# Mean of the squares by a constant matrix, and a stacked low-rank gate, in a hybrid decoder layer

## The chip, the cores and the metric

The kernel runs on one core of a Trainium2 chip. The metric is the device time of one execution, in microseconds (us). Engines are named as in the profile: PE (TensorE's products) and PEld (its weight loads), DVE (VectorE), ACT (ScalarE), POOL (GpSimd), SP (SyncE, which issues nearly all DMAs).

## What is computed

One decoder layer on 256 tokens of 1024 channels, float32: a mixer (gated linear attention beside causal pooling), a layer norm, a mixture of 64 experts with a shared one, a second layer norm. The change touches two places of the attention branch:

```python
# the gate: a product of rank 16, then one up to 512 channels
log_decay = log_sigmoid(einsum('bsr,rk->bsk', g_lr, w_gate_up) + b_gate) / 16
...
# each head's output (256 channels) over the root of its mean square
def rms_norm(x, g):
    y = x * lax.rsqrt(jnp.square(x).mean(-1, keepdims=True) + RMS_EPS)
    return y * g
o = rms_norm(o, gla_norm_g).reshape(B, S, GLA_DV)
o = o * silu(r)
```

## The kernel before

**Stages.** The mixer comes first (to some 215 us of the span), then routing, then 32 steps of two experts each, whose weights stream in through rings of 1 MB buffers. All instructions are issued in the order in which the program writes them, engine by engine; no scheduler moves them.

**Projections.** The input weights come in 22 chunks of 256 columns (q, k, v, r, u, ga, gb; buffers `w_0` to `w_21`), each handled as halves. A half is first *split*: ACT writes a rounded copy `sh` (type float32r, L296), DVE the rest `sl` (L297). Then PE runs 24 products on it: L300 (`sh` with the rounded x), L301 (`sh` with x's rest), L302 (`sl` with the rounded x). The loop `run` issues the split of a half two places ahead of its products (`LOOK = 2`), and `between` behind each half's products issues one step of the background generators: `pool_steps` and the chain `gla_steps`, `out_steps`, `gate_steps`. So work of the attention and pooling branches stands in every engine's queue between the splits and products of the halves.

**The gate.** Behind chunk q0 comes the piece `g`: `split_to(wg, ...)` makes the rounded and the rest part of the rank-16 weights side by side (`wgs`, 32 columns), and `rank_mm` (L615) multiplies them with both parts of x: 16 float32r products into 32 rows of `pg` (L620, L621). ACT copies these to `glr` in float32. After the next half, `gla_steps` multiplies `wgu` (the up weights, loaded twice so that 32 rows add both parts) with `glr`: four products in plain float32 (L366), which the trace shows as 8 passes, into `plog`.

**The heads' norms.** `out_steps` (L488) has a step for each of the four heads: products `po` (L503, L504); then `square_sums` of the head before: two float32 products with the squares `sq` as weights and a column of ones, giving one number for each token, tokens on partitions (`psq`, L495); ACT squares (L508), POOL adds the two halves of the channels (L509), ACT writes the scaled output `oT` (L513). After the last head ACT takes the root of the 128x8 sums (L516) and DVE the reciprocal (L517). Since the outputs lie with channels on partitions, the roots are then spread over all partitions by products with the identity, four for two heads (`prs`, L535), and DVE multiplies `oT` by silu(r) (L527) and by `prs` (L528), which it reads from PSUM. `pool_steps` goes on beside this: DVE's `pl` (L557 to L559), one product `pm` (L553), DVE's `mx`.

**POOL at the start.** Its queue holds a cast of the identity, a cast `trib` of constants that a DMA brings (L280), memsets of `A0`, `A1` (L345, L346) and, from `gla_steps`, of `B` (L373).

Of the kernel before, what the change touches and what calls it, by code (L numbers as in the profile page):

```python
# [5 lines left out]
FT = mybir.dt.float32  # L6
FR = mybir.dt.float32r
BF = mybir.dt.bfloat16
I32 = mybir.dt.int32
AF = mybir.ActivationFunctionType  # L10
# [3 lines left out]
T, D = 256, 1024  # L14
H, DK, DV = 4, 128, 256
# [95 lines left out]
def body(ctx, tc, A, out, dbg=lambda *a: None, stop=None):  # L111
    nc = tc.nc
    ctx.enter_context(tc.manual_schedule())
    PE, V, S, G = nc.tensor, nc.vector, nc.scalar, nc.gpsimd
# [94 lines left out]
    ident = cst[:, C_ID:C_ID + 128]  # L209
# [24 lines left out]
    right = tc.alloc_tile_pool(name="right", bufs=1, side="right")  # L234
    gla = tc.alloc_tile_pool(name="gla", bufs=1)
    onesb = right.tile([128, 128], BF, name="onesb")
    cst1 = right.tile([128, C_COLS - C_KEPT], FT, name="cst1")

    def cst_of(c, n):
# [4 lines left out]

    x = ring1.tile([128, 2048], FT, name="x", tag="w1", bufs=NR1).rearrange("p (t d) -> p t d", t=2)
    wg = gla.tile([128, 8, 16], FT, name="wg")
    wgu = gla.tile([32, 512], FT, name="wgu")
    wgrp = right.tile([128, 4, 128], FT, name="wgrp")
    nc.scalar.dma_start(ident, A["cst"][:, C_ID:C_ID + 128])
    halves = [slice(0, 512), slice(512, 1024)]  # L250
# [5 lines left out]
    ring.midway = lambda: load_x(1)  # L256
    ring.issue(ring1, "w1", NR1)
    nc.sync.dma_start(wg, w_in[:, 3072:3088].rearrange("(k p) c -> p k c", p=128))
    for n in range(2):
        nc.sync.dma_start(wgu[16 * n:16 * n + 16], A["w_gate_up"][0])  # L260
    nc.sync.dma_start(bgate, A["b_gate"][0].rearrange("(h p) -> p h", p=128))
    ring.issue(ring1, "w1", NR1)
    nc.sync.dma_start(cst1, A["cst"][:, C_KEPT:])
# [11 lines left out]
    V.memset(eps_rms, RMS_EPS)  # L275
    V.memset(eps_ln, LN_EPS)
    V.memset(onesb, 1.0)
    V.memset(ones1, 1.0)
    G.tensor_copy(identb, ident)
    G.tensor_copy(trib, cst_of(C_TRI, 128))  # L280
# [14 lines left out]
    def split_to(src, hi, lo, eng=V):  # L295
        S.activation(hi, src, AF.Copy)  # L296
        eng.tensor_sub(lo, src, hi.bitcast(FT))  # L297
# [39 lines left out]

    qT = gla.tile([128, H, T], FT, name="qT")
    kT = gla.tile([128, H, T], FT, name="kT")
    glr = gla.tile([32, T], FT, name="glr")  # L340
    wgs = gla.tile([128, 8, 2, 16], FR, name="wgs")
    v = right.tile([128, 2, D], FT, name="v")
    A0 = right.tile([128, H, 256], FT, name="A0")
    A1 = right.tile([128, H, 128], FT, name="A1")
# [12 lines left out]
    pools, L = {}, {}  # L357

    def gla_steps():
        yield  # L360
        xb = gla.tile([128, H, T], FT, name="E", bufs=2)
        for hp in range(2):
            p = bank("b", (2, T), "plog")
            for h2 in range(2):
                h = 2 * hp + h2
                PE.matmul(p[:, h2], wgu[:, 128 * h:128 * (h + 1)], glr, start=True, stop=True)  # L366
            for h2 in range(2):
                h = 2 * hp + h2
                V.tensor_scalar(xb[:, h], p[:, h2], bgate[:, h:h + 1], None, op0=OP.add)
# [116 lines left out]
        yield  # L486

    def out_steps():  # L488
        oTs = {}
        psq = bank("b", (2, H), "psq")  # L490
        rs = right.tile([128, 2, H], FT, name="rs")

        def square_sums(h):
            for t in range(2):
                PE.matmul(psq[:, t, h:h + 1], L["sq", h][:, 128 * t:128 * (t + 1)], one_c,  # L495
                          start=h == 0 and t == 0, stop=True, skip_group_check=True)

        yield ("v", 3)
        for h in range(H):
# [13 lines left out]
                S.activation(oT[:, c], p[:, c], AF.Copy, scale=gnorm[:, c:c + 1])  # L513
            yield
        square_sums(H - 1)
        S.activation(rs, psq, AF.Sqrt, bias=eps_rms, scale=1.0 / DV)  # L516
        V.reciprocal(rs, rs)  # L517
        yield ("r", 3)
        og, prs = {}, {}
        for i in range(H + 2):  # L520
            if i >= 2:
                hs = slice(2 * i - 4, 2 * i - 2)
                split_to(og[i - 2], L["ogh"][:, hs], L["ogl"][:, hs], eng=G)
            if 1 <= i <= H:
                h = i - 1
                og[h] = right.tile([128, 2, T], FT, name="og", tag="og", bufs=2)
                V.tensor_mul(og[h], oTs[h], rT[:, 2 * h:2 * h + 2])  # L527
                V.tensor_mul(og[h], og[h], prs[h // 2][:, h % 2, None, :].to_broadcast([128, 2, T]))  # L528
            if i < H:
                S.activation(rT[:, 2 * i:2 * i + 2], rT[:, 2 * i:2 * i + 2], AF.Silu)  # L530
                if i % 2 == 0:
                    prs[i // 2] = bank("b", (2, T), "prs")
                    for h2 in range(2):
                        for t in range(2):
                            PE.matmul(prs[i // 2][:, h2, 128 * t:128 * (t + 1)],  # L535
                                      rs[:, t, i + h2:i + h2 + 1].to_broadcast([128, 128]), ident,
                                      start=True, stop=True)
            yield

    def pool_steps():  # L540
# [74 lines left out]
    def rank_mm():  # L615
        pg = bank("b", (T,), "pg")

        for k in range(8):
            w = wgs[:, k].rearrange("p a r -> p (a r)")
            PE.matmul(pg[:32], w, xTh[:, k], start=k == 0, stop=False)  # L620
            PE.matmul(pg[:32], w, xTl[:, k], start=False, stop=k == 7)  # L621
        S.activation(glr, pg[:32], AF.Copy)

    pieces = []
    for name, c, _ in chunk_cols:
        st = {}
        parts = 4 if (name, c) == ("q", 0) else 2
        for part in range(parts):
            if len(pieces) == 1:
                pieces.append((("x", 0, True), lambda: None, lambda: x_part(1)))  # L630
            pieces.append(((name, c, part == parts - 1),) + proj_piece(name, c, part, parts, st))
        if (name, c) == ("q", 0):
            pieces.append((("g", 0, 1), lambda: split_to(wg, wgs[:, :, 0], wgs[:, :, 1]), rank_mm))

    def done(key):
        finished.add(key)
# [695 lines left out]
```

## Time and profile before

| | |
|---|---|
| time before, median of 3 runs | 690.85 us (690.08 to 690.96) |
| the profiled execution: its own time, its span | 691.21 us, 689.4 us |
| PE, PEld busy share of the span | 97%, 68% |
| DVE, ACT, POOL | 42%, 33%, 10% |
| mean DMA rate over the span | 351 GB/s |
| chain that ended last, by engine | PE 25%, DMA 13%, DVE 1% |

The profiled execution is one run under the hardware profiler; its span runs from the first to the last instruction, and its own time holds 1.8 us around that. The shares are means over stages that differ, so a stage is read from its own stretch. Matmul durations overlap (they are pipelined), so what a product costs is read from one start to the next.

### The profile page before, as it was taken

The numbers are of one execution on the slowest core, as the hardware profiler recorded it, in microseconds if no ns is written. First come the engines' busy times: TensorE is split into PE (matmuls) and PEld (weight loads), VectorE is DVE, ScalarE is ACT, GpSimd is POOL, SyncE is SP. The second block draws the span as 40 slices with busy tenths as digits, with TensorE's granted clock in tenths as the row PEclk, the third lists the DMA queues.
The fourth block names the chain that finished last, engine by engine and source line by source line (L and its number), as shares of the span: only waits on it lengthen the run. The fifth ranks groups of instructions, "written<-read, shape, count | busy, mean of one in ns | idle before, by whom it ended". The sixth has DMA issues, their size and how long they took to land. (4 is left out here: it accounts for less than half of the span.)

```text
span 689.4 us, 13660 instructions
## 1 busy us (share of the span) xinstructions
PE 668.5 (97%) x5940; PEld 471.8 (68%) x5940; DVE 287.8 (42%) x458; ACT 227.8 (33%) x348; POOL 66.8 (10%) x53
## 2 busy tenths in 40 slices
PE   8999999999999999999999999999999999798994
PEld 8999999999999756556546546556645655464531
DVE  3698845946676522123123123324431321231216
ACT  4654546674445213123123113311311321131222
POOL 1064404600002000000000002100000000100001
PEclk9999999999999999999999999999999999999997
DMA  9995533499677999999999999999999999999991
GB/s 283 308 349 163 180 123 124 142 385 420 249 265 299 348 421 381 422 420 419 418 419 421 420 419 419 411 420 421 418 420 422 418 421 417 421 419 417 408 328 64
DMA packets 66885, 242.02 MB, mean 351 GB/s; under 512 B 7012, under 2 KB 36452, under 8 KB 43016
## 3 DMA queue, kind: packets, MB, share of 16 engines
q1 hardware_dynamic: 66680, 241.07, 89.2%
q8 instruction: 47, 0.77, 0.5%
q10 hardware_dynamic: 144, 0.07, 0.1%
q14 instruction: 14, 0.11, 0.0%
HBM read 240.07 MB, written 1.05 MB: 350 GB/s over the span
## 5 line engine op out<-in xcount | busy, mean ns | idle before, releaser
L1033 PE MATMUL pgu<-w,xg 128*64 128x256 f32 x1840 | 222.4, 381 | 1.3 <-DMA w<-in_w_exp_gate 1.3
L1033 PEld LDWEIGHTS pgu<-w,xg 128*64 128x64 f32 x1840 | 138.7, 137 | 86.1 <-ACT Y L1063 11.7
L1058 PE MATMUL py<-w,ht 128*32 128x512 f32 (+1 forms) x912 | 120.2, 580 | 1.8 <-DMA w<-in_w_exp_down 1.4
L297 DVE TENSOR_TENSOR sl<-w,sh 128x1024 fp32r<-128x1024 f32 (+1 forms) x63 | 80.3, 1281 | 40.3 <-ACT sh L296 40.1
L1040 DVE TENSOR_TENSOR h<-sg,pgu 128x256 f32<-128x256 f32 x32 | 13.5, 422 | 191.3 <-ACT sg L1039 147.0
L1064 DVE SCALAR_TENSOR_TENSOR Y<-py,gsl,Y 128x512 fp32r<-128x512 f32 (+1 forms) x66 | 48.5, 735 | 102.1 <-ACT Y L1063 102.0
L1063 ACT ACTIVATE Y<-py,gsl 128x512 fp32r<-128x512 f32 (+1 forms) x66 | 44.5, 674 | 116.1 <-PE py L1058 116.1
L300 PE MATMUL proj<-xTh,sh 128*128 128x256 f32 x288 | 82.0, 285 | 0.3 <-ACT sh L296 0.3
L301 PE MATMUL proj<-xTl,sh 128*128 128x256 f32 x288 | 80.6, 280 | 0.0
L302 PE MATMUL proj<-xTh,sl 128*128 128x256 f32 x288 | 80.3, 279 | 0.2 <-DVE sl L297 0.2
L1039 ACT ACTIVATE sg<-pgu 128x256 f32<-128x256 f32 x32 | 12.3, 384 | 201.6 <-PE pgu L1033 201.6
L296 ACT ACTIVATE sh<-w 128x1024 fp32r<-128x1024 f32 (+1 forms) x63 | 64.2, 1027 | 32.8 <-PE proj L302 12.6
L1058 PEld LDWEIGHTS py<-w,ht 128*32 128x32 f32 x912 | 30.5, 109 | 55.0 <-issue 46.9
L300 PEld LDWEIGHTS proj<-xTh,sh 128*128 128x128 f32 x288 | 54.1, 188 | 1.1 <-ACT sh L296 0.5
L301 PEld LDWEIGHTS proj<-xTl,sh 128*128 128x128 f32 x288 | 54.1, 188 | 0.3 <-DVE xTl L297 0.2
L302 PEld LDWEIGHTS proj<-xTh,sl 128*128 128x128 f32 x288 | 54.0, 187 | 0.4 <-DVE sl L297 0.4
L1058 PE MATMUL py<-xTh,ht 128*32 128x512 f32 x80 | 36.3, 594 | 0.0
L1033 PE MATMUL pgu<-xTl,xg 128*64 128x256 f32 x128 | 29.2, 381 | 3.8 <-DMA xTl<-in_w_exp_up 3.8
L786 DVE TENSOR_SCALAR xg<-pgat,cols_sb 128x512 f32<-128x512 f32 x32 | 25.7, 809 | 13.9 <-PE pgat L914 11.4
L914 PE MATMUL pgat<-P,xl 128*128 128x256 f32 x128 | 30.6, 283 | 0.3 <-DVE xl L950 0.3
L788 ACT ACTIVATE xg<-pgat,cols_sb 128x512 f32<-128x512 f32 x32 | 24.7, 778 | 17.3 <-PE pgat L914 17.3
L914 PE MATMUL pgat<-P,xh 128*128 128x256 f32 x128 | 30.3, 283 | 0.0
(271 smaller groups left out, 950.7 us busy)
## 6 DMA issues: line engine op xcount, KB each, us to landing
w<-in_w_exp_gate SPq DMA_DIRECT2D x62, 1024.0 KB, 15.9
w<-in_w_exp_up SPq DMA_DIRECT2D x53, 1024.0 KB, 16.8
w<-in_w_exp_down SPq DMA_DIRECT2D x47, 1024.0 KB, 19.8
w<-in_w_in SPq DMA_DIRECT2D x21, 1024.0 KB, 7.0
xTl<-in_w_exp_up SPq DMA_DIRECT2D x7, 1024.0 KB, 15.6
w<-in_w_exp_down SPq DMA_DIRECT2D x12, 512.0 KB, 14.8
xTh<-in_w_exp_down SPq DMA_DIRECT2D x5, 1024.0 KB, 19.8
w<-in_w_gla_up SPq DMA_DIRECT2D x4, 1024.0 KB, 10.8
```

The lines of the kernel that those rows point to most:

```text
L296: S.activation(hi, src, AF.Copy)
L297: eng.tensor_sub(lo, src, hi.bitcast(FT))
L300: PE.matmul(o, ah, bh, start=start, stop=False, skip_group_check=shared_bank)
L301: PE.matmul(o, ah, bl, start=False, stop=False, skip_group_check=shared_bank)
L302: PE.matmul(o, al, bh, start=False, stop=stop, skip_group_check=shared_bank)
L786: V.tensor_scalar(dst, p, g1T[:, k:k + 1], b1T[:, k:k + 1], op0=OP.mult, op1=OP.add)
L788: S.activation(dst, p, AF.Identity, bias=b1T[:, k:k + 1], scale=g1T[:, k:k + 1])
L914: PE.matmul(p[k][:, t].rearrange("p e s -> p (e s)"), part[:, t, k], P8[o][:, t].rearrange("p e s -> p (e s)"), start=part is xh, stop=par ...
L1033: PE.matmul(p[64 * c:64 * c + 64, g], xg[:, k, e].rearrange("p t s -> p (t s)"), w[c][:, k], start=k == 0, stop=k == 7, tile_position=(0, ...
L1058: PE.matmul(p[32 * c:32 * c + 32], HT[2 * q + c // 2][:, j, c % 2, t], ring.get(li["down", 4 * q + c])[:, j, cs], start=j == 0, stop=j == ...
L1063: S.activation(hi, p, AF.Copy, scale=g)
L1064: V.scalar_tensor_tensor(lo, p, g, hi.bitcast(FT), op0=OP.mult, op1=OP.subtract)
```

## The change

The gate: the up weights are loaded six times by one DMA, into 96 rows. The first product's weights are written three times side by side (POOL copies them, in the new `split_rank`), so that it gives the low-rank rows three times, in 96 rows. Of these the first 64 are kept rounded (`glr`, now float32r) and the last 32 hold the rest; of the up weights rows 32 to 63 hold the rest and the others the rounded part (`wgr`). One float32r product over 96 rows then adds the three partial products.

The norms: a 128x128 matrix of 1/256 is the weight, and a head's squares move past it, so that the mean of each token arrives on all partitions at once. Two heads share a bank; after the second, ACT takes the root and DVE the reciprocal of 128x512, in place of rows of `A0` that are no longer needed, and DVE multiplies by them from there. The products that spread the roots are gone.

```diff
--- before.py
+++ after.py
@@ -234,6 +234,7 @@
     right = tc.alloc_tile_pool(name="right", bufs=1, side="right")
     gla = tc.alloc_tile_pool(name="gla", bufs=1)
     onesb = right.tile([128, 128], BF, name="onesb")
+    mean = right.tile([128, 128], FT, name="mean")
     cst1 = right.tile([128, C_COLS - C_KEPT], FT, name="cst1")
 
     def cst_of(c, n):
@@ -244,7 +245,8 @@
 
     x = ring1.tile([128, 2048], FT, name="x", tag="w1", bufs=NR1).rearrange("p (t d) -> p t d", t=2)
     wg = gla.tile([128, 8, 16], FT, name="wg")
-    wgu = gla.tile([32, 512], FT, name="wgu")
+    wgu = gla.tile([96, 512], FT, name="wgu")
+    wgr = gla.tile([96, 512], FR, name="wgr")
     wgrp = right.tile([128, 4, 128], FT, name="wgrp")
     nc.scalar.dma_start(ident, A["cst"][:, C_ID:C_ID + 128])
     halves = [slice(0, 512), slice(512, 1024)]
@@ -256,8 +258,8 @@
     ring.midway = lambda: load_x(1)
     ring.issue(ring1, "w1", NR1)
     nc.sync.dma_start(wg, w_in[:, 3072:3088].rearrange("(k p) c -> p k c", p=128))
-    for n in range(2):
-        nc.sync.dma_start(wgu[16 * n:16 * n + 16], A["w_gate_up"][0])
+    six = bass.AP(tensor=A["w_gate_up"].tensor, offset=A["w_gate_up"].offset, ap=[[0, 6], [512, 16], [1, 512]])
+    nc.sync.dma_start(wgu, six)
     nc.sync.dma_start(bgate, A["b_gate"][0].rearrange("(h p) -> p h", p=128))
     ring.issue(ring1, "w1", NR1)
     nc.sync.dma_start(cst1, A["cst"][:, C_KEPT:])
@@ -275,6 +277,7 @@
     V.memset(eps_rms, RMS_EPS)
     V.memset(eps_ln, LN_EPS)
     V.memset(onesb, 1.0)
+    V.memset(mean, 1.0 / DV)
     V.memset(ones1, 1.0)
     G.tensor_copy(identb, ident)
     G.tensor_copy(trib, cst_of(C_TRI, 128))
@@ -337,8 +340,8 @@
 
     qT = gla.tile([128, H, T], FT, name="qT")
     kT = gla.tile([128, H, T], FT, name="kT")
-    glr = gla.tile([32, T], FT, name="glr")
-    wgs = gla.tile([128, 8, 2, 16], FR, name="wgs")
+    glr = gla.tile([96, T], FR, name="glr")
+    wgs = gla.tile([128, 8, 3, 2, 16], FR, name="wgs")
     v = right.tile([128, 2, D], FT, name="v")
     A0 = right.tile([128, H, 256], FT, name="A0")
     A1 = right.tile([128, H, 128], FT, name="A1")
@@ -363,7 +366,7 @@
             p = bank("b", (2, T), "plog")
             for h2 in range(2):
                 h = 2 * hp + h2
-                PE.matmul(p[:, h2], wgu[:, 128 * h:128 * (h + 1)], glr, start=True, stop=True)
+                PE.matmul(p[:, h2], wgr[:, 128 * h:128 * (h + 1)], glr, start=True, stop=True)
             for h2 in range(2):
                 h = 2 * hp + h2
                 V.tensor_scalar(xb[:, h], p[:, h2], bgate[:, h:h + 1], None, op0=OP.add)
@@ -486,14 +489,18 @@
         yield
 
     def out_steps():
-        oTs = {}
-        psq = bank("b", (2, H), "psq")
-        rs = right.tile([128, 2, H], FT, name="rs")
+        oTs, psq, prs = {}, {}, {}
 
         def square_sums(h):
-            for t in range(2):
-                PE.matmul(psq[:, t, h:h + 1], L["sq", h][:, 128 * t:128 * (t + 1)], one_c,
-                          start=h == 0 and t == 0, stop=True, skip_group_check=True)
+
+            if h % 2 == 0:
+                psq[h // 2] = bank("b", (2, T), "psq")
+            PE.matmul(psq[h // 2][:, h % 2], mean, L["sq", h], start=True, stop=True)
+            if h % 2:
+
+                prs[h // 2] = rs = A0[:, h - 1:h + 1]
+                S.activation(rs, psq[h // 2], AF.Sqrt, bias=eps_rms)
+                V.reciprocal(rs, rs)
 
         yield ("v", 3)
         for h in range(H):
@@ -513,10 +520,8 @@
                 S.activation(oT[:, c], p[:, c], AF.Copy, scale=gnorm[:, c:c + 1])
             yield
         square_sums(H - 1)
-        S.activation(rs, psq, AF.Sqrt, bias=eps_rms, scale=1.0 / DV)
-        V.reciprocal(rs, rs)
         yield ("r", 3)
-        og, prs = {}, {}
+        og = {}
         for i in range(H + 2):
             if i >= 2:
                 hs = slice(2 * i - 4, 2 * i - 2)
@@ -528,13 +533,6 @@
                 V.tensor_mul(og[h], og[h], prs[h // 2][:, h % 2, None, :].to_broadcast([128, 2, T]))
             if i < H:
                 S.activation(rT[:, 2 * i:2 * i + 2], rT[:, 2 * i:2 * i + 2], AF.Silu)
-                if i % 2 == 0:
-                    prs[i // 2] = bank("b", (2, T), "prs")
-                    for h2 in range(2):
-                        for t in range(2):
-                            PE.matmul(prs[i // 2][:, h2, 128 * t:128 * (t + 1)],
-                                      rs[:, t, i + h2:i + h2 + 1].to_broadcast([128, 128]), ident,
-                                      start=True, stop=True)
             yield
 
     def pool_steps():
@@ -615,11 +613,19 @@
     def rank_mm():
         pg = bank("b", (T,), "pg")
 
+
         for k in range(8):
-            w = wgs[:, k].rearrange("p a r -> p (a r)")
-            PE.matmul(pg[:32], w, xTh[:, k], start=k == 0, stop=False)
-            PE.matmul(pg[:32], w, xTl[:, k], start=False, stop=k == 7)
-        S.activation(glr, pg[:32], AF.Copy)
+            w = wgs[:, k].rearrange("p n a r -> p (n a r)")
+            PE.matmul(pg[:96], w, xTh[:, k], start=k == 0, stop=False)
+            PE.matmul(pg[:96], w, xTl[:, k], start=False, stop=k == 7)
+        S.activation(glr, pg[:96], AF.Copy)
+        V.tensor_sub(glr[64:96], pg[64:96], glr[64:96].bitcast(FT))
+        S.activation(wgr, wgu, AF.Copy)
+        V.tensor_sub(wgr[32:64], wgu[32:64], wgr[32:64].bitcast(FT))
+
+    def split_rank():
+        split_to(wg, wgs[:, :, 0, 0], wgs[:, :, 0, 1])
+        G.tensor_copy(wgs[:, :, 1:3], wgs[:, :, 0:1].to_broadcast([128, 8, 2, 2, 16]))
 
     pieces = []
     for name, c, _ in chunk_cols:
@@ -630,7 +636,7 @@
                 pieces.append((("x", 0, True), lambda: None, lambda: x_part(1)))
             pieces.append(((name, c, part == parts - 1),) + proj_piece(name, c, part, parts, st))
         if (name, c) == ("q", 0):
-            pieces.append((("g", 0, 1), lambda: split_to(wg, wgs[:, :, 0], wgs[:, :, 1]), rank_mm))
+            pieces.append((("g", 0, 1), split_rank, rank_mm))
 
     def done(key):
         finished.add(key)
```

On POOL, at the start of the program: `trib` is the cast of constants, `A_210`/`A_211` are A0 and A1, `wgs` the first product's weights. Before:

```order
L279 CAST identb<-cst 128x128 [waits DMAHW0_49]
L280 CAST trib<-cst_97 128x128 [waits DMAHW4_49]
L345 MEMSET A_210 128x1024
L346 MEMSET A_211 128x512
L373 MEMSET B 128x1024
L458 ISA
```

and now:

```order
L282 CAST identb<-cst 128x128 [waits DMAHW0_49]
L283 CAST trib<-cst_98 128x128 [waits DMAHW3_49]
L348 MEMSET A_212 128x1024
L349 MEMSET A_213 128x512
L628 COPY wgs<-wgs 128x8x64 [waits DVE_49]
L376 MEMSET B 128x1024
```

A copy of 128x8x64 stands behind the two memsets, and the memset of `B` behind it; the first of the gate's products now waits for POOL where it waited for DVE.

On DVE, from the third head's step to the second step of the pool branch (`w_15`, `w_16` are the second and third ga chunk). Before:

```order
L297 TENSOR_TENSOR sl<-w_15_917,sh 128x1024 [waits DMAHW2_49,Activation_49]
L297 TENSOR_TENSOR sl<-w_15_917,sh 128x1024 [waits PE_49,Activation_49]
L557 SCALAR_TENSOR_TENSOR pl<-sw,uT 128x256 [waits Pool_49]
L558 TENSOR_TENSOR pl<-sw,cst_97 128x16 [waits DVE_49]
L559 TENSOR_TENSOR pl<-pl,uT 128x16 [waits DVE_49]
L517 RECIPROCAL rs<-rs 128x8 [waits Activation_49]
L297 TENSOR_TENSOR sl<-w_16_1021,sh 128x1024 [waits DMAHW3_49,PE_49,Activation_49]
L557 SCALAR_TENSOR_TENSOR pl<-sw,uT 128x256 [waits Pool_49]
L558 TENSOR_TENSOR pl<-sw,cst_97 128x16 [waits DVE_49]
L559 TENSOR_TENSOR pl<-pl,uT 128x16 [waits DVE_49]
L297 TENSOR_TENSOR sl<-w_16_1021,sh 128x1024 [waits PE_49,Activation_49]
```

and now:

```order
L503 RECIPROCAL A_212<-A_212 128x512 [waits Activation_49]
L300 TENSOR_TENSOR sl<-w_15_923,sh 128x1024 [waits DMAHW1_49,Activation_49]
L300 TENSOR_TENSOR sl<-w_15_923,sh 128x1024 [waits PE_49,Activation_49]
L555 SCALAR_TENSOR_TENSOR pl<-sw,uT 128x256 [waits Pool_49]
L556 TENSOR_TENSOR pl<-sw,cst_98 128x16 [waits DVE_49]
L557 TENSOR_TENSOR pl<-pl,uT 128x16 [waits DVE_49]
L503 RECIPROCAL A_212<-A_212 128x512 [waits Activation_49]
L300 TENSOR_TENSOR sl<-w_16_1027,sh 128x1024 [waits DMAHW2_49,PE_49,Activation_49]
L555 SCALAR_TENSOR_TENSOR pl<-sw,uT 128x256 [waits Pool_49]
L556 TENSOR_TENSOR pl<-sw,cst_98 128x16 [waits DVE_49]
L557 TENSOR_TENSOR pl<-pl,uT 128x16 [waits DVE_49]
L300 TENSOR_TENSOR sl<-w_16_1027,sh 128x1024 [waits PE_49,Activation_49]
```

A reciprocal of 128x512 stands before the first `sl` of `w_15`, and the one behind the first `pl` triple, ahead of `w_16`, grows from 128x8 to 128x512.

## Rows read from the trace of the kernel before

**Rows 1.** Busy time of the engines by stretch: us, PE, PEld, DVE, ACT, POOL, PEclk, DMA share, GB/s

```profile
112.00:140.00 28.00, 28.00 (x234) 27.79 (x234) 23.70 (x34) 19.69 (x29) 13.76 (x13) 1.00 0.46 156
180.00:215.00 35.00, 35.00 (x231) 32.04 (x230) 23.79 (x30) 15.23 (x23) 5.10 (x2) 1.00 0.62 215
240.00:600.00 360.00, 354.85 (x3018) 205.66 (x3014) 99.37 (x174) 80.33 (x138) 9.65 (x6) 1.00 1.01 418
```

**Rows 2.** Timeline of PE late in the experts: start us, us, engine, line, what [idle before]

```profile
656.97 0.43 PE L1033 MATMUL pgu<-xTl,xg 128*64 128x256 f32 x1 [1.20 <-DMA xTl<-in_w_exp_up]
```

**Rows 3.** Timeline of PE around the gate's two products

```profile
15.51 0.28 PE L620 MATMUL pg<-xTh,wgs 128*32 128x256 f32 x1
...
17.35 0.28 PE L300 MATMUL proj<-xTh,sh 128*128 128x256 f32 x1
...
19.95 0.28 PE L302 MATMUL proj<-xTh,sl 128*128 128x256 f32 x1
20.16 1.99 PE L366 MATMUL plog<-glr,wgu 32*128 32x256 f32 x8
...
22.30 0.28 PE L301 MATMUL proj<-xTl,sh 128*128 128x256 f32 x1
```

**Rows 4.** Timeline of POOL in the same stretch

```profile
14.57 0.29 POOL L280 CAST trib<-cst 128x128 bf16<-128x128 f32 x1 [10.56 <-DMA cst<-in_cst]
...
15.69 0.53 POOL L346 MEMSET A<- 128x512 f32 x1
16.16 0.96 POOL L373 MEMSET B<- 128x1024 f32 x1
```

**Rows 5.** POOL's largest plain copy, from the costliest groups: busy us, mean ns

```profile
L919 POOL CAST xh<-x 128x1024 fp32r<-128x1024 f32 x1 | 2.1, 2149 | 72.4 <-DVE x L779 72.4
```

**Rows 6.** Columns as in rows 1, the microsecond in which the constants land

```profile
14.00:15.00 1.00, 1.00 (x11) 1.00 (x10) 0.00 (x0) 0.95 (x1) 0.42 (x2) 1.00 1.10 347
```

**Rows 7.** Timeline of PE: square sums of one head, and one spreading of the roots

```profile
99.62 0.50 PE L495 MATMUL psq<-small,sq 128*128 128x1 f32 x4
99.99 0.36 PE L300 MATMUL proj<-xTh,sh 128*128 128x256 f32 x1
...
115.34 0.59 PE L553 MATMUL pm<-pl,wgrp 128*128 128x256 f32 x2
115.77 1.05 PE L535 MATMUL prs<-cst,rs 128*128 128x128 f32 x8
116.58 0.36 PE L300 MATMUL proj<-xTh,sh 128*128 128x256 f32 x1
```

**Rows 8.** Timeline of DVE from the last head to the second gb half

```profile
113.02 0.41 DVE L557 SCALAR_TENSOR_TENSOR pl<-sw,uT 128x256 f32<-128x256 f32 x1
...
113.67 0.18 DVE L559 TENSOR_TENSOR pl<-pl,uT 128x16 f32<-128x16 f32 x1
...
115.42 1.23 DVE L297 TENSOR_TENSOR sl<-w,sh 128x1024 fp32r<-128x1024 f32 x1 [0.74 <-ACT sh L296]
...
118.32 1.23 DVE L297 TENSOR_TENSOR sl<-w,sh 128x1024 fp32r<-128x1024 f32 x1 [0.91 <-ACT sh L296]
...
133.42 1.61 DVE L297 TENSOR_TENSOR sl<-w,sh 128x1024 fp32r<-128x1024 f32 x1
```

**Rows 9.** Timeline of PE: first product that uses that last sl

```profile
136.05 0.28 PE L302 MATMUL proj<-xTh,sl 128*128 128x256 f32 x1
```

**Rows 10.** Reciprocals of eight elements and of one: duration ns min/median/max, first and last start us

```profile
L517 DVE RECIPROCAL rs<-rs x1: 203/203/203, 114.5 to 114.5; 128x8 f32<-128x8 f32 x1
L778 DVE RECIPROCAL mv<-mv x2: 164/164/165, 208.0 to 215.1; 128x1 f32<-128x1 f32 x2
L1261 DVE RECIPROCAL mv<-mv x2: 151/158/164, 679.1 to 682.2; 128x1 f32<-128x1 f32 x2
```

**Rows 11.** The two multiplications of a head's og, columns as in rows 10

```profile
L527 DVE TENSOR_TENSOR og<-oT,rT x4: 684/758/1107, 120.6 to 131.9; 128x512 f32<-128x512 f32 x4
L528 DVE TENSOR_TENSOR og<-og,prs x4: 686/687/689, 121.4 to 132.8; 128x512 f32<-128x512 f32 x4
```

## The prediction

> **What bounds the kernel now.** I read the stretches first, then the chain that ended last, then the timelines of the places the change touches. In the stretches [rows 1] PE is busy 28.00 of 28 us between 112 and 140, and 35.00 of 35 between 180 and 215, while the DMA engines are at 0.46 and 0.62 of their time. From 240 to 600 the DMA share is 1.01. So the mixer is bound by PE, and the experts by the weight stream, which PE meets again at the end: at 656.97 it has stood 1.20 us for a transfer [rows 2]. The stream starts late because its buffers come free as PE gets on, so each microsecond that PE gains or loses in the mixer should move the whole end by as much. The change is priced in PE's time before 215 us, and another engine's work counts only where PE waits for it. DVE is the one to watch: busy 23.70 of 28 us where the heads' roots are used [rows 1].
>
> **The second product of the gate.** Before, it is 8 float32 passes. From the last projection product ahead of it (19.95) to the second one behind it (22.30) PE needs 2.35 us [rows 3]. After, it is four products of 128x256 in one pass each. The first product of the gate is in that form and takes 1.84 us for 16, from 15.51 to 17.35, so 0.115 each [rows 3]. With the two projection products that stand in the 2.35 us, six of them take 0.69. The saving is 2.35 - 0.69 = **1.66 us**. The first product keeps its 16 instructions and 256 columns; it writes 96 rows instead of 32. The projection piece behind it writes 128 rows and starts its 24 products between 17.35 and 19.95, 2.60/23 = 0.113 each [rows 3], so I cost the added rows at nothing.
>
> **The copies of its weights.** They are made on POOL, behind two memsets and a cast of constants that waits for a load. The constants land at 14.57, and POOL is free only at 16.16, when it begins the memset of B [rows 4]; the new copy takes that place. PE wants the weights at 15.51 [rows 3], so it must wait. Two terms stand on bounds. The copy is 128x512. A memset of that shape takes 0.53 [rows 4]; the only copy to the product's type, of twice the length, takes 2.15, half of which is 1.08 [rows 5]. I take 0.8, the middle. The gate's up weights are loaded six times in one DMA instead of twice in two, 128 KB more, ahead of the constants in a queue whose engines are already full (share 1.10, 347 GB/s [rows 6]): 0.38 us later, or nothing if the one DMA issue saved lets the queue start as much earlier. I take 0.38. Then PE starts at 16.16 + 0.38 + 0.8 = 17.34, a wait of **1.83 us**, between 1.18 and 2.11. If POOL were free, the wait would vanish.
>
> The new ACT and DVE steps (the copy of the low-rank rows in 96 rows, the rounded weights, two subtractions) lie between the two products, where PE works on a projection piece from 17.35 to 20.16, 2.8 us [rows 3]. Three of them in series at the 0.69 of a 128x512 multiplication [rows 11] are 2.1 us: covered, with 0.7 to spare; without cover they would cost what exceeds 2.8. The memset of the mean matrix stands before the warm-up products, which only fill time before x lands: nothing, and at worst 0.53 [rows 4].
>
> **The mean and the roots.** A head's sums take PE 0.37 us before (99.62 to 99.99 [rows 7]). After, they are one float32 product of 128x256, two passes; such a pair takes 0.43 (115.34 to 115.77 [rows 7]). Four heads: 4 x 0.06 = **+0.24 us**. Spreading the roots, 0.81 us (115.77 to 116.58 [rows 7]), is removed; it occurs twice: **-1.62 us**. So PE wins 1.38 us here if nobody makes it wait. The ACT roots grow from 128x8 to two of 128x512, and the order has as many table loads as before; ACT is busy 19.69 of 28 us [rows 1], so I cost them at nothing.
>
> DVE pays. Its reciprocals grow from 8 elements to 512, twice. The row of 8 took 203 ns, those of one element 164 and at best 151 [rows 10]. The slope is 39/7 = 5.6 or 52/7 = 7.4 ns an element, so one reciprocal is between 3.0 and 3.95 us, if the slope holds so far beyond; I take **3.4**. If the slope were an artefact, the floor is the 0.69 of a plain 128x512 operation [rows 11]. The Trainium skill ("VectorE: DVE Perf Modes", "First, the fixed hardware budget") says that a reciprocal is an iterated divide with a repeat count of 8, not one pass. An estimate from that page, 8 cycles at its 0.96 GHz for 512 elements, is 4.3 us, which would add 0.9 us to the sum below; the rows agree that it is no single pass, and I stay with their value.
>
> The first reciprocal falls into a stretch where DVE waits. The second follows the pool step that ends at 113.85 (113.67 + 0.18); then come an sl of 1.23 and the next pool step of 0.83 (113.02 to 113.85), some 2.0 us, before the sl that starts at 118.32 [rows 8]. That one would start at 113.85 + 3.4 + 2.0 = 119.25, 0.93 later. From there DVE goes on without a break to the sl that starts at 133.42 and takes 1.61, ending at 135.03 [rows 8]. PE uses it at 136.05 [rows 9], so 1.02 us are spare. PE comes 1.38 earlier. The four multiplications by the root now read it where oT and rT lie, no longer from a PSUM bank; with the bank they took 686 to 689 ns, the neighbours without it 758 in the median and up to 1107 [rows 11]. I add 4 x 0.07 = 0.28. PE waits 0.93 + 0.28 + 1.38 - 1.02 = **1.57 us**, and the win of 1.38 becomes a loss of 0.19. The Trainium skill ("SBUF — State Buffer", "Who interferes with whom") has the rule behind the wider row: a DVE operation with two SBUF inputs and a GpSimd one lock each other out. Rows 11 agree with it, and by the rule alone, each of the four held up as the worst neighbour was (0.42), the sum would be 1.4 higher.
>
> **The sum.** -1.66 + 1.83 + 0.19 = +0.36 us on the profiled execution of 691.21 (span 689.4). That execution stands 0.36 above the median of 690.85; on the median the forecast is **691.2 us**, no change that can be told: 0.2%, about what a measurement of this kernel can tell from none, is 1.4 us.
>
> **Rivals.**
> - *DVE becomes the bound of the heads' roots, slower.* With 3.95 us for a reciprocal and 0.25 for each held-up multiplication the delay is 1.48 + 1.0; PE waits 1.48 + 1.0 + 0.36 = 2.84, a loss of 1.46 here; with the gate's +0.17, +1.6: **692.5**. It decides once DVE is over 2.3 us later than now at the sl of 133.42. For it: the steeper slope, and a DVE without breaks there. Against: POOL is busy only 13.76 of 28 us [rows 1].
> - *DVE has room and POOL is quick, faster.* A reciprocal at 0.69 and no later root leave the 1.38 nearly whole; a copy of 0.53 and constants that land no later make the gate's wait 1.18, so 0.48 won. Together up to -1.86: **689.0**. For it: only 7 elements carry the slope. Against: both short ends must hold; with a short reciprocal alone it is -1.21, within no change.
> - *The gate's products don't change their form.* If the second product still ran two passes each, its whole saving of 1.66 is gone: **692.9**. The declared type is the one of the first product, so this is unlikely.
>
> **How the numbers follow.** Forecast, with both waits of roughly these sizes: same 0.55. DVE as the bound 0.29, since a little more on the reciprocals and the held-up multiplications passes +1.4, and the form unchanged 0.02: slower 0.31. The fast corner: 0.14. The range runs from the fast corner, 689.0, to the slow rival with the gate's longest wait (2.11, +0.28) and a little of the worst lockout, 693.0.
>
> **What would show it.** Right: PE idle ahead of the gate's first product, released by POOL, near 1.8 us; the second product in some 0.5 us with no wait; no spreading products; two DVE reciprocals of 3 to 4 us; PE idle for DVE's sl between 118 and 137, some 1.5 us; the expert stage shifted as a whole. Wrong if the reciprocals take under 1 us, if PE does not wait for POOL, or if the experts' stretch itself changes length by over 0.5 us.

## The result, and the profile after

The changed kernel takes **695.28 us** in the median of 5 runs (694.13 to 695.88), the kernel before 690.85 (690.08 to 691.08) beside it: ratio 1.0065, 95% interval 1.0054 to 1.0076, so 3.7 to 5.3 us slower. Forecast were 691.2, between 689.0 and 693.0. The profiled execution took 695.88 us; its span is 694.1 against 689.4.

The busy time of the engines by stretch, in the columns of [rows 1] (the granted clock of PE is the third number from the end):

```profile
15.00:23.00 8.00, 4.78 (x29) 4.58 (x28) 3.03 (x4) 3.45 (x6) 3.15 (x5) 0.79 1.10 348
18.00:19.00 1.00, 0.51 (x2) 0.51 (x3) 0.83 (x1) 0.14 (x1) 1.00 (x2) 0.59 1.10 348
19.00:20.00 1.00, 1.00 (x7) 1.00 (x6) 0.52 (x1) 0.00 (x0) 0.33 (x1) 0.50 1.11 349
20.00:21.00 1.00, 1.00 (x7) 1.00 (x6) 0.00 (x0) 0.00 (x0) 0.00 (x0) 0.50 1.10 348
22.00:23.00 1.00, 1.00 (x10) 1.00 (x10) 0.46 (x2) 0.97 (x3) 0.00 (x0) 1.00 1.10 348
...
112.00:140.00 28.00, 26.15 (x206) 25.07 (x204) 26.24 (x33) 18.12 (x29) 13.67 (x14) 1.00 0.35 113
240.00:600.00 360.00, 354.77 (x3034) 207.49 (x3032) 100.41 (x178) 80.71 (x139) 9.91 (x6) 1.00 1.01 417
```

The experts are as before: PE 354.77 of 360, DMA share 1.01 [rows 1]. The loss sits in the two places of the change, at the gate and where the heads' roots are used. Between the gate's two products the timelines of POOL and of PE answer to [rows 4] and [rows 3]. POOL:

```profile
16.17 0.29 POOL L283 CAST trib<-cst 128x128 bf16<-128x128 f32 x1 [12.08 <-DMA cst<-in_cst]
...
17.77 0.67 POOL L628 CAST wgs<-wgs 128x512 fp32r<-128x512 f32 x1
```

PE:

```profile
18.49 0.53 PE L619 MATMUL pg<-xTh,wgs 128*96 128x256 f32 x1 [3.22 <-POOL wgs L628]
18.82 0.41 PE L620 MATMUL pg<-xTl,wgs 128*96 128x256 f32 x1
19.03 0.41 PE L619 MATMUL pg<-xTh,wgs 128*96 128x256 f32 x1
...
21.84 0.28 PE L303 MATMUL proj<-xTh,sh 128*128 128x256 f32 x1
...
24.55 0.28 PE L305 MATMUL proj<-xTh,sl 128*128 128x256 f32 x1
24.66 0.64 PE L369 MATMUL plog<-glr,wgr 96*128 96x256 f32 x4
25.14 0.28 PE L303 MATMUL proj<-xTh,sh 128*128 128x256 f32 x1
25.26 0.28 PE L304 MATMUL proj<-xTl,sh 128*128 128x256 f32 x1
```

The constants land at 16.17 instead of 14.57, so the copy ends late and PE stands 3.22 us. Their load is already issued late, at 9.60 instead of 8.46. SP's issues, before and after:

```profile
8.46 1.12 SPq L263 DMA_DIRECT2D cst<-in_cst  x1
```

```profile
9.60 0.58 SPq L265 DMA_DIRECT2D cst<-in_cst  x1
```

Then the 16 products take 21.84 - 18.49 = 3.35 us, where they took 1.84. The granted clock in the four short windows above says why. Behind the idle 3.22 us PE is granted 0.50, the 1.2 GHz level, and is back at 1.00 from 22 us on. The second product takes 0.48 (24.66 to 25.14) and starts without a wait, as it should.

In the heads' stage, DVE's groups between 104 and 142 us (busy us, mean ns, idle before) answer to [rows 10, 11]; the second list is what PE waited for from 90 to 215 us (us in total, times, longest):

```profile
L503 DVE RECIPROCAL A<-A 128x512 f32<-128x512 f32 x2 | 6.7, 3350 | 1.6 <-ACT A L502 1.6
L532 DVE TENSOR_TENSOR og<-oT,rT 128x512 f32<-128x512 f32 x4 | 4.2, 1040 | 0.0
L533 DVE TENSOR_TENSOR og<-og,A 128x512 f32<-128x512 f32 x4 | 4.1, 1013 | 0.1
```

```profile
PE pm L551 <- DVE pl L557: 1.2, 2, 0.8
PE proj L305 <- DVE sl L300: 1.1, 2, 0.9
```

To compare kernels whatever their start, I use two distances in their timelines: **A**, from the first projection product of q (8.00 before) to the first head's `po` (94.19 before), holds the gate; **B**, from there to the copy of the first gb chunk (138.84 before), holds the heads.

| kernel | A, us | B, us |
|---|---|---|
| before | 86.19 | 44.65 |
| after | 89.70 | 46.16 |

So the gate costs 3.51 and the heads 1.51 us. The first q product came 0.51 us earlier in this execution (7.49), which leaves the 4.5 us by which everything behind lies later. B is steady: the eight profiles with the old norms have 44.65 to 44.67. A is not: four kernels below with one and the same gate (e3, e5, e6, e7) have 85.57 to 86.49, so a difference under 0.9 us in A alone can't be told.

### The profile page after: what moved, and what is told of

Its sections match the earlier page's. It is cut to its first block, busy times and chain, and to the rows that moved or that the text cites. A ratio compares the mean times of both kernels' runs of the same rounds, so it can differ in the third digit from the quotient of the medians.

```text
span 694.1 us, 13607 instructions
## 1 busy us (share of the span) xinstructions
PE 666.5 (96%) x5912; PEld 470.6 (68%) x5912; DVE 295.9 (43%) x462; ACT 229.3 (33%) x350; POOL 66.7 (10%) x54
## 3 DMA queue, kind: packets, MB, share of 16 engines
HBM read 240.21 MB, written 1.05 MB: 348 GB/s over the span
```

## The experiments

Ratios are to the kernel before on the same chip, with 95% intervals. The runs were spread over several chips, on which the kernel before takes 690.48 to 690.96 us, so kernels are compared by their ratios.

### The parts alone

`e1_gate_only` and `e2_norms_only` are the kernel before with one half of the change's diff each.

> The kernel before with the gate part of the change alone. Theory A, two separate losses (gate: 3.2 us of waiting and about 1.4 us at half the granted clock against 1.66 us saved, net about +3.0; heads' stage about +1.5): 693.8 us, the shift at the first kT product the same as in the changed kernel and none added after 94 us. Rival B, one cause at the gate and the later 1.5 us only its knock-on on transfers: 695.3 us. Rival C, the heads' stage alone decides: 690.9 us or less.

> The kernel before with the norms part of the change alone. Theory A: 692.3 us, with nothing changed before 94 us and the two reciprocals of 3.35 us on VectorE. Rival B: 690.9 us. Rival C: 695 us.

Gate alone: 694.19 us, ratio 1.0044 (1.0031 to 1.0057); A is 89.99, B 44.65. Norms alone: 692.01 us, 1.0018 (1.0009 to 1.0027); A is 86.27, B 46.14. Theory A holds: two losses, each in its own distance, adding up to 1.0062 of the 1.0065.

### The wait and the clock

`e3_copy_first` moves one line of POOL's queue, `e4_six_later` one DMA, and `e9_warm_wait` fills PE's wait:

```diff
# e3
-    G.tensor_copy(trib, cst_of(C_TRI, 128))
...
         G.tensor_copy(wgs[:, :, 1:3], wgs[:, :, 0:1].to_broadcast([128, 8, 2, 2, 16]))
+        G.tensor_copy(trib, cst_of(C_TRI, 128))
# e4
-    nc.sync.dma_start(wgu, six)
...
     nc.sync.dma_start(cst[:, C_IOTA:], A["cst"][:, C_IOTA:C_KEPT])
+    nc.sync.dma_start(wgu, six)
# e9, in rank_mm ahead of the 16 products
+        for _ in range(45):
+            PE.matmul(pg[:, :128], onesb, onesb, start=True, stop=True)
```

> The changed kernel with GpSimd's cast of trib behind the copy of wgs, so that the copy no longer waits for the constants. Theory A: the first product does not wait, the granted clock stays at 1.00, the gate gives its 1.66 us back: 690.6 us. Rival: what delays the first product is the weights' own landing or split, or the clock falls for another reason: 694 to 695 us.

> The changed kernel with the six-fold load of w_gate_up issued behind the two loads of the constants. If the six-fold load is what made the constants land 1.6 us later: they land near 14.6 us, the first product waits about 1.7 us; the clock then stays at 1.00 (as behind the gaps of 1.2 to 1.3 us in the kernel before) and the time is 692.4 us, or still falls and it is 693.8 us. Rival: the constants are late for another reason (the ring's loads beside them) and it stays at 695.3 us.

> The changed kernel with 45 products of ones in PE's wait for the copy (about 3.0 us), so that PE is busy while it waits. If the half granted clock behind the wait comes of PE's idleness: granted clock 1.00 at the first product, its pitch 0.115 us, and the time is 1.4 us less: 693.9 us. If the clock falls for another reason: 695.3 us or more.

**e9**: 694.34 us, 1.0059 (1.0042 to 1.0076). The interval does not tell it from the changed kernel; the trace does. PE's timeline:

```profile
15.08 2.69 PE L616 MATMUL pg<-onesb 128*128 128x128 bf16 x45
18.38 0.36 PE L621 MATMUL pg<-xTh,wgs 128*96 128x256 f32 x1 [0.62 <-POOL wgs L630]
18.58 0.28 PE L622 MATMUL pg<-xTl,wgs 128*96 128x256 f32 x1
18.70 0.28 PE L621 MATMUL pg<-xTh,wgs 128*96 128x256 f32 x1
```

and one window:

```profile
19.00:20.00 1.00, 1.00 (x11) 1.00 (x10) 0.40 (x1) 0.00 (x0) 0.22 (x1) 1.00 1.11 350
```

The first product starts as late as in the changed kernel (18.38), but the clock is 1.00 and the pitch (from one product's start to the next) 0.12 instead of 0.21; A falls from 89.70 to 88.26. The half clock came of PE's idleness and cost 1.44 us; the stretch from the first product of the gate to the second alone shrinks by 1.37 (from 6.17 to 4.80).

**e4**: 692.71 us, 1.0037 (1.0020 to 1.0054), A 85.81. The constants land at 14.85, PE waits 1.05, and the clock stays at 1.00. POOL, then PE:

```profile
14.85 0.29 POOL L283 CAST trib<-cst 128x128 bf16<-128x128 f32 x1 [10.74 <-DMA cst<-in_cst]
```

```profile
17.11 0.36 PE L619 MATMUL pg<-xTh,wgs 128*96 128x256 f32 x1 [1.05 <-POOL wgs L628]
17.31 0.28 PE L620 MATMUL pg<-xTl,wgs 128*96 128x256 f32 x1
```

So the place of the six-fold load delays the constants. (The first q product came late here, at 8.57, which the time has and A has not.)

**e3**: 691.81 us, 1.0018 (1.0009 to 1.0027), A 86.13. POOL, then PE:

```profile
13.13 0.61 POOL L627 CAST wgs<-wgs 128x512 fp32r<-128x512 f32 x1 [7.67 <-DVE wgs L299]
15.92 0.29 POOL L628 CAST trib<-cst 128x128 bf16<-128x128 f32 x1 [2.18 <-DMA cst<-in_cst]
```

```profile
15.13 0.28 PE L618 MATMUL pg<-xTh,wgs 128*96 128x256 f32 x1
...
17.77 0.38 PE L304 MATMUL proj<-xTh,sl 128*128 128x256 f32 x1 [0.38 <-DVE sl L299]
20.46 0.70 PE L368 MATMUL plog<-glr,wgr 96*128 96x256 f32 x4
```

The wait and the half clock are gone, 3.57 us of A. But theory A wanted 690.6: nothing is left of the second product's saving (the ratio is that of e2, which has the old gate), and a new wait for DVE stands at 17.77. Where it went is the last group of experiments.

### The heads

All three start from `e3_copy_first`:

```diff
# e5: the heads are multiplied by the root itself
-                V.reciprocal(rs, rs)
# e6, ahead of every second Silu
+                    rs = prs[i // 2]
+                    prs[i // 2] = bank("b", (2, T), "prs")
+                    S.activation(prs[i // 2], rs, AF.Copy)
# e7
-                S.activation(rs, psq[h // 2], AF.Sqrt, bias=eps_rms)
-                V.reciprocal(rs, rs)
+                S.activation(rs, psq[h // 2], AF.Ln, bias=eps_rms)
# e7, for both pairs ahead of the first Silu
+                    S.activation(rs, rs, AF.Exp, scale=-0.5)
```

> e3_copy_first with the two reciprocals on VectorE left out (the heads are multiplied by the root instead of its inverse). Theory L, the length of the two reciprocals (6.7 us on an engine without idle time from 113 to 137 us) is the heads' loss: PE's waits there (2.5 us) go and PE keeps the 1.4 us net that psq and prs gave back: 688.9 us. Rival H, the loss is VectorE held by GpSimd now that the factor lies in SBUF: some 1.0 to 1.5 us of waits stay, 690.5 to 691.5 us.

> e3_copy_first with the inverse root copied by ScalarE into a PSUM bank (0.6 us, twice) before the heads read it. Rival H: og<-og,factor goes back from a mean of 1.01 us to 0.69 us, four times, and 1.3 us less on VectorE makes 690.6 us. Theory L: the durations may fall, but the reciprocals stay ahead of everything; the holds move to the next operations and the time stays within 0.5 us of e3_copy_first: 691.8 us.

> e3_copy_first with the inverse root made on ScalarE alone (Ln instead of Sqrt, then Exp of -0.5 times it), nothing of it on VectorE; ScalarE gets one more table load of 1.28 us and two Exp of about 0.7 us. Theory L: VectorE loses 6.7 us and the waits go: 689.3 us. Rival: the 2.7 us in front of ScalarE's split at 116 us hold PE up by 1 to 1.5 us instead: 690.5 us. Rival H: 691 us.

| kernel | us | ratio (95%) | B, us |
|---|---|---|---|
| e3 | 691.81 | 1.0018 (1.0009 to 1.0027) | 46.03 |
| e5, no reciprocals | 689.94 | 0.9990 (0.9981 to 1.0000) | 44.35 |
| e6, root in PSUM | 690.22 | 0.9991 (0.9981 to 1.0000) | 44.86 |
| e7, Ln and Exp on ACT | 692.29 | 1.0020 (1.0010 to 1.0030) | 46.47 |

In e6, DVE's groups and PE's waits, as above:

```profile
L502 DVE RECIPROCAL A<-A 128x512 f32<-128x512 f32 x2 | 6.7, 3350 | 1.6 <-ACT A L501 1.6
L532 DVE TENSOR_TENSOR og<-og,prs 128x512 f32<-128x512 f32 x4 | 2.7, 686 | 0.1
```

```profile
PE pm L554 <- DVE pl L560: 1.1, 2, 0.6
PE proj L304 <- DVE sl L299: 0.2, 1, 0.2
```

And in e5, whose results are not those of the layer, PE's only wait:

```profile
PE proj L304 <- DVE sl L299: 0.9, 1, 0.9
```

The reciprocals are unchanged in e6, yet 4 x (1013 - 686) ns = 1.3 us less on DVE bring back 1.17 of B. In e5, 6.7 us less bring back 1.68, although the multiplications stay held up at a mean of 1044 ns. Neither theory holds alone: **each cause has a wait of its own**. In e3, as in the changed kernel, PE waits 1.2 us for `pl` and 1.1 for `sl`. Without the reciprocals the wait for `pl` is gone and 0.9 of that for `sl` stays; with the root in PSUM the wait for `pl` stays (1.1) and that for `sl` falls to 0.2. So the two should add: an estimate from both gains, 46.03 - 1.68 - 1.17 = 43.18, lies 1.47 under the B of the kernel before. No run takes both away.

The mean of 1013 ns hides two cases. In the changed kernel the first multiplication runs while POOL is idle, the other three (1.11 to 1.13 us) beside a subtraction on POOL:

```profile
125.81 0.69 DVE L533 TENSOR_TENSOR og<-og,A 128x512 f32<-128x512 f32 x1
130.15 1.11 DVE L533 TENSOR_TENSOR og<-og,A 128x512 f32<-128x512 f32 x1
```

```profile
129.91 0.80 POOL L300 TENSOR_TENSOR mxl<-mx,mxh 128x256 fp32r<-128x256 f32 x1 [1.10 <-ACT mxh L299]
```

The Trainium skill ("SBUF — State Buffer", "Who interferes with whom") has a rule for it: a DVE operation with two SBUF inputs and a GpSimd one that reads SBUF shut each other out. The traces agree with it, at 0.43 us for each of the three, and so does e6: three of its four run beside the same subtractions, with one input in PSUM, and take 686 ns.

e7 goes the way of its rival, and further. The wait for `pl` grows to 1.5, because a DVE split ahead of it stands 2.92 us for ACT:

```profile
PE pm L552 <- DVE pl L558: 1.5, 2, 1.2
```

```profile
118.97 1.22 DVE L299 TENSOR_TENSOR sl<-w,sh 128x1024 fp32r<-128x1024 f32 x1 [2.92 <-ACT sh L298]
```

ACT's split for it starts at 117.90, where the same one starts at 115.38 in e5: the table load and the Exp ahead of ACT's splits took over as the late step. The wait for `sl` stays at 1.1, with all four multiplications held up (1116 ns in the mean).

### Where the second product's saving went

With the wait gone, the gate should have won 1.5 us. The candidates: the splits that the change adds between the two products, the six-fold load, and the pitch of the projection products behind, which is longer. e8, e10, e12 and e13 have the changed norms, the others the old ones.

```diff
# e8 = e3 with these two steps on POOL behind the copy of wgs
-        S.activation(wgr, wgu, AF.Copy)
-        V.tensor_sub(wgr[32:64], wgu[32:64], wgr[32:64].bitcast(FT))
+        G.tensor_copy(wgr, wgu)
+        G.tensor_sub(wgr[32:64], wgu[32:64], wgr[32:64].bitcast(FT))
# e10 = e8 with e6's lines; e11 = e8 with the old norms
# e12 = e3 with e4's and e6's lines; e14 = the same gate, old norms
# e13 = e12 with, behind the last of the four second products:
+                PE.matmul(bank("b", (1,), "one"), ident, one_c, start=True, stop=True)
# e15 = before, with wgu loaded by the six-fold DMA and used in 32 rows
# e16 = e3's gate, old norms, wgu loaded twice as before
+    for n in range(1, 3):
+        G.memset(wgu[32 * n:32 * n + 32], 0.0)
# e17 = before, with the second product in three fp32r passes on 32 rows;
# POOL makes the two parts of wgu (wgh, wgl) ahead of trib
-                PE.matmul(p[:, h2], wgu[:, 128 * h:128 * (h + 1)], glr, start=True, stop=True)
+                mm3(p[:, h2], wgh[:, hc], wgl[:, hc], glr, gll, True, True)
```

> e3_copy_first with the split of w_gate_up on GpSimd, behind the copy of wgs, instead of on ScalarE and VectorE behind the first product. In e3_copy_first 0.7 us of the 1.5 us saved at the second product were lost between the two products, 0.4 of them waiting for VectorE's split. If the two added splits there are the cause: the second product starts 0.4 to 0.7 us earlier after the first and the time is 0.5 us under e3_copy_first (0.8 us over the kernel before). If the later landing of the weights is the cause: the same as e3_copy_first (1.3 us over).

> e8_wgu_on_pool with the inverse root copied into PSUM. If the parts add up: 1.2 us (the measured stage of e6_root_in_psum against e3_copy_first) under e8_wgu_on_pool, 0.4 to 1.2 us under the kernel before. Rival, nothing left to gain once one of the two is mended: equal to e6_root_in_psum, 0.7 us under the kernel before.

> The kernel before with the mended gate of e8_wgu_on_pool and its own norms. If the mended gate keeps what the shorter second product saves: 1.0 to 1.5 us under the kernel before (689.4 us by 690.7) and faster than e10_both by up to 0.5 us. Rival, the saved 1.5 us are taken back by the later splits and by a longer pitch of the products that follow: within 0.3 us of the kernel before.

> The changed kernel with three mends: the copy ahead of trib, the six-fold load behind the constants, the inverse root copied into PSUM. If the six-fold load's place is what takes the saved time back: the weights' split at 15.3 us starts at 14.0 us again, VectorE's low half comes in time, and the time is 0.5 to 0.6 us under e10_both, 0.6 to 1.2 us under the kernel before. Rival, the load delays the weights behind it instead and the wait moves to the second product: no faster than e10_both.

> e12_six_last with one more float32 product, of one column, behind the gate's second products. In all kernels with the stacked second product the 144 products that follow come at a pitch of 0.118 us, in those with the float32 one at 0.113 us. If the float32 product just ahead sets the level: the pitch goes to 0.113 us up to the first product of k, 0.6 us come back and the product costs 0.3 to 0.5 us: within 0.3 us of e12_six_last, but 0.6 us less from there to the first gs. If something else sets it (the transfers beside, the weights' places): the pitch stays at 0.118 us and the time is 0.3 to 0.5 us more.

> The kernel before with the gate part and two mends (copy ahead of trib, six-fold load behind the constants), its own norms. If the gate is mended by them: 0.6 to 1.2 us under the kernel before. Rival, the saved time is taken back by the pitch and the weights anyway: within 0.3 us of it, as e11_gate_old_norms.

> The kernel before with the six-fold load of w_gate_up alone (its first 32 rows are used as before, all products as before). If the load's 128 KB more and its slow transfer are what takes the saved time back: the constants land 1.4 us later, the weights' split goes from 14.05 to 15.3 us, PE waits 0.4 to 0.6 us for it behind the first product, and the time is 0.5 to 1.0 us over the kernel before. If the longer pitch does it: the pitch stays at 0.113 us behind the float32 products and the time is within 0.3 us of the kernel before.

> The kernel before with the gate part and the copy ahead of trib, but w_gate_up loaded twice as before and the 64 other rows set to zero (this leaves out the small parts of the second product). If the load takes the saved time back: no wait behind the first product, constants at 14.6 us, and the time 0.8 to 1.4 us under the kernel before. If the pitch does: it is 0.118 us from the first product to the first gs, and the time is 0.2 to 0.7 us under.

> The kernel before with its second gate product as three fp32r products over the 32 rows it has (high times high, low times high, high times low), no six-fold load, no copy of wgs, nothing of the norms. The second product's four float32 products of about 2.0 us become twelve at 0.117 us, 1.4 us, and a bubble of 0.2 us goes: if nothing but the load took the saving of the changed gate back, 0.6 to 0.8 us under the kernel before. Rival, GpSimd's split of w_gate_up ahead of trib or VectorE's low half of the first product come late: within 0.2 us of it.

> The kernel before itself, profiled once more. If the pitch of the products between the gate and the first gs is the kernel's own: 0.113 us again. If it differs from one execution to the next (then it takes no part in the differences between kernels): 0.118 us, with the first product of q at another place than 8.0 us.

The last column is the distance from the projection product behind the second product to the first `gs`:

| kernel | us | ratio (95%) | A | to gs |
|---|---|---|---|---|
| before | 690.85 | | 86.19 | 16.63 |
| e18, before again | 690.53 | one run | 85.80 | 16.63 |
| e8 | 692.14 | 1.0015 (1.0006 to 1.0024) | 85.93 | 17.37 |
| e10 | 690.88 | 0.9998 (0.9989 to 1.0007) | 85.66 | 17.17 |
| e11 | 690.75 | 0.9996 (0.9987 to 1.0005) | 86.25 | 17.07 |
| e12 | 690.71 | 0.9999 (0.9990 to 1.0008) | 86.34 | 18.39 |
| e13 | 690.48 | 1.0001 (0.9991 to 1.0010) | 85.73 | 17.64 |
| e14 | 690.46 | 0.9997 (0.9988 to 1.0006) | 86.89 | 18.26 |
| e15, load alone | 691.58 | 1.0013 (1.0004 to 1.0022) | 87.13 | 17.06 |
| e16, without the load | 689.81 | 0.9986 (0.9977 to 0.9995) | 84.96 | 16.96 |
| e17 | 690.45 | 0.9999 (0.9990 to 1.0008) | 86.01 | 17.06 |

**The splits** are not what PE waits for: e11, which has none of the two steps between the products, still waits 0.56 for DVE.

```profile
17.69 0.39 PE L302 MATMUL proj<-xTh,sl 128*128 128x256 f32 x1 [0.56 <-DVE sl L297]
```

What they cost beside that is not settled: e8's ratio is close to e3's, but the intervals leave room for the 0.5 us in question. The distance between the gate's two products is no test either. It is 4.85 in e8 and 5.33 in e3, but 5.17, 5.53 and 4.71 in e5, e6 and e7, whose gate is e3's; it is shortest in e7, where the first q product came last (7.87), as it would be if the weights land at a time of their own and a later PE waits less for them.

**The six-fold load** is the main cause. Alone, in the kernel before, it costs 0.9 us (e15); without it the mended gate, less the small parts of its second product, wins 1.0 (e16). In e15 the weights of q's second chunk reach ACT at 15.74 instead of 14.05, and PE waits behind the first product. ACT, then PE:

```profile
15.74 1.06 ACT L296 ACTIVATE sh<-w 128x1024 fp32r<-128x1024 f32 x1 [3.27 <-DMA w<-in_w_in]
```

```profile
18.11 0.38 PE L302 MATMUL proj<-xTh,sl 128*128 128x256 f32 x1 [0.46 <-DVE sl L297]
```

What it costs is more than its bytes. Where the queue should be full behind it, the DMA engines are partly idle. Before, then e15, in the columns of [rows 1]:

```profile
10.00:12.00 2.00, 2.00 (x20) 2.00 (x19) 0.91 (x3) 1.28 (x3) 0.00 (x0) 1.00 1.08 334
```

```profile
10.00:12.00 2.00, 2.00 (x20) 2.00 (x19) 1.39 (x3) 1.42 (x4) 0.00 (x0) 1.00 0.87 241
```

The changed kernel has 0.86 and 234 GB/s there, e16, without the load, 1.09 and 329. No run shows what in the load does it.

Moving it back (e12, e14) moves the wait, as the rival had it: the next weights are late instead, PE waits 0.28 and 0.32 us for DVE's halves at 29.3 and 32.7 in e14, and the last column grows to 18.3. ACT had waited 1.72 us for a transfer there at 19.69:

```profile
19.69 1.06 ACT L296 ACTIVATE sh<-w 128x1024 fp32r<-128x1024 f32 x1 [1.72 <-DMA w<-in_w_in]
```

e13 has the load in the same place and neither of these waits, and ends level too, so one profile each does not show that the wait must move there.

**The pitch** goes with some 0.3 to 0.4 us more (16.96 in e16, 17.06 in e15 and e17, against 16.63). From the second product to `gs` it was 0.113 us nearly all the way in the kernel before both times, and in e2; with the gate or the load changed it is 0.117 to 0.118. e18, then e15, first product and first `gs`:

```profile
21.91 0.38 PE L300 MATMUL proj<-xTh,sh 128*128 128x256 f32 x1
...
38.54 0.65 PE L391 MATMUL gs<-qT,kT 128*32 128x32 f32 x52
```

```profile
22.82 0.39 PE L300 MATMUL proj<-xTh,sh 128*128 128x256 f32 x1
...
39.88 0.31 PE L391 MATMUL gs<-qT,kT 128*32 128x32 f32 x13
```

That the float32 product sets it, as e13 supposed, fell twice: e13's stays at 0.117, and e15 has all float32 passes of the kernel before and 0.117 too. (e13's last column is 0.75 under e12's, as forecast, but by the 0.40 and 0.32 us that PE waited for DVE in e12.) Nor is it fixed for a kernel: before runs at 0.118 up to 16 us, then at 0.113, in e18 from 13 us, and both are at 0.118 again from 35.5 to 39.7. What sets it stays open. e17, without the load, saves 0.32 at the second product and loses 0.43 to the pitch.

No version that computes everything beats the kernel before by more than can be told: e10 to e14 and e17 end level with it, and e6's gain of 0.6 us has an interval that ends at nothing.

## Why the prediction was wrong

**The bound** was right: PE's loss in the mixer moved the end by as much, and the experts' stretch kept its length.

**The saving of 1.66** at the second product was right in place: between the prediction's own two points 2.35 became 0.71 (24.55 to 25.26), 1.64; the new ACT and DVE steps were covered, as forecast. That it would stay was wrong; a load that shares its queue with the weights was priced for the constants alone, not for the weights behind it.

**The wait of 1.83, which was to lie between 1.18 and 2.11**, is the step that failed. The copy was sized rightly (0.67 for 0.8), the landing was not: 0.38 was the bytes over the full rate, and 1.60 was measured. The rate did not hold (234 GB/s from 10 to 12 us), and one DMA issue fewer did not let SP start the constants' load earlier: it started 1.14 later. And the wait's price is not its length: the two clock levels were in no term. 3.22 us of wait and 1.44 us of half clock stand against 1.83, 2.8 of the 4.1 us by which the median misses; the heads are the other 1.3. The sentence that without a busy POOL the wait would vanish held (e3).

**The reciprocals** were right: 3.35 for 3.4. The estimate of 4.3 from the Trainium skill ("VectorE: DVE Perf Modes", "First, the fixed hardware budget") is too high; the measurement decides.

**The four held-up multiplications** were the other failed term: 0.07 each forecast, 0.33 measured. The median of the neighbours was the wrong row to take, since POOL's subtractions run beside three of these steps; the rule of the lock, priced in the prediction at 0.42 each, fits those three (0.43). The multiplications by silu(r) beside them grew as well, from a mean of 827 to 1040 ns, which no term had. PE's wait for `pl` (1.2) was not in the forecast either: the delay by the second reciprocal was followed to the next `sl`, not to the `pm` product that needs the `pl` behind it. The stage cost 1.51 us instead of 0.19. That this is nearly the 1.46 of the first rival is luck: its reciprocals were too long, its multiplications too short, and the wait for `pl` was not in it. The mean product and the spreading that it removes came out about as priced: psq and the way to the second product behind it take 0.55 (102.64 to 103.19) after 0.57, where +0.06 was forecast, and no spreading is left.

## What to carry to other kernels

A wait on PE has two prices, its length and the clock behind it; where the profile shows a long idle stretch, read the granted clock after it before costing the products that follow. A small load ahead of others in a queue costs what the loads behind it wait, which can be more than its bytes, so follow each of them to the engine that needs it, and look for a version without the load. Before an operand moves from PSUM to SBUF, see what GpSimd runs at that time; on an engine that had no break there, 1.3 us more on four operations cost 1.17. And when an engine is delayed, follow the delay to everything that waits for it, not only to the largest user.

## What the runs showed of the hardware

- PE idle for 3.22 us was granted 0.50 behind it, and 1.00 again from 22 us on; idle for 1.05 us (e4), or kept busy with products of ones (e9), it stayed at 1.00.
- One DMA that reads the same 16 rows six times (192 KB), where two of 32 KB had stood, made the constants behind it land 1.6 us later (1.7 in e15); by its 128 KB more at 347 GB/s it would be 0.4. From 10 to 12 us the DMA engines moved 234 and 241 GB/s instead of 334, and SP issued the constants' load 1.1 and 1.3 us later.
- In the changed kernel DVE's multiplication by the root (128x512, both inputs in SBUF) took 0.69 us while POOL was idle and 1.11 to 1.13 beside a subtraction on POOL; with the root in PSUM (e6) it took 0.69 beside the same subtractions.
- Projection products of one form, at a granted clock of 1.00, run at one of two pitches, 0.113 or 0.118 us, and change between them within one execution.
